# Hybrid diffusion step on one core: the first norm's product taken before the modulations, scale, shift and split after them

## Chip, cores and metric

The kernel runs on one core of one Trainium2 chip. The metric is device microseconds (us) of one execution. A kernel's time is the median of several runs. Before the change it is 1882.99 us, the median of three runs from 1879.08 to 1884.51.

## What is computed

One inference step of a two-layer backbone, for 512 latent tokens and 128 context tokens of width 1024. Each sub-layer takes an RMS norm of the residual stream, then a scale and a shift that come from a conditioning vector through a linear map (the modulations), then a mixer, an output projection and a convolutional gated MLP. The change lies in the first of these norms:

```
def modulation(cvec, w_mod, b_mod):
    m = jax.nn.silu(cvec) @ w_mod + b_mod
    return jnp.split(m[:, None, :], 6, axis=-1)

sh1, sc1, g1, sh2, sc2, g2 = modulation(cvec, p['w_mod'][i], p['b_mod'][i])
h = rmsnorm(x, p['norm_mix'][i]) * (1.0 + sc1) + sh1
# even layer: DeltaNet heads and a Hyena long convolution
proj = h @ p['ev_w_in'][j]
filt = hyena_filters(L, p, j)
```

`rmsnorm` is x times the reciprocal root of the mean square over the 1024 channels, times a gain. The Hyena filters don't depend on the tokens. They come from a small network on positions and are then taken to the frequency domain.

## The kernel before

**Layout.** Channels lie on the 128 partitions and tokens along the free dimension: 642 columns, of which 0 to 511 are latent tokens, 512 and 513 a gap, and 514 to 641 context tokens. The 1024 channels are 8 blocks of 128 (index d), two to a tile, so the input is four tiles `x0`. Work on all tokens is done in two halves, columns 0 to 383 and 384 to 641 (`HALVES`); the second half has two parts with a scale and shift each (`HPARTS`). The large products go three times through TensorE (`mm3`, L310 to L312): the activation and the weight are each split into a rounded high part and the rest, the low part. So each activation needs a high tile (a ScalarE cast, L429) and a low tile (a subtraction, L430).

**The prologue.** L888 makes the generator `filt` of the Hyena filters, and L889 to L912 are the code around the change. A loop of 16 steps takes the shift and scale maps of layer 0 (`mod_chunk`, L212): each step loads 512 KB of `w_mod` and multiplies it by the conditioning columns. In the same loop the four `x0` tiles are loaded, the squares of x are summed over the blocks into `acc` (`sq_acc`, L437 and L440), and `filt` is advanced 12 times. After the loop, `settle` ends the last `mod_finish`: a ScalarE copy (L223), a transpose on TensorE (L227) and the addition of the bias on VectorE (L230). `mod_scale` (L276) makes the scale `scl`. Then for each half:

- `norm_stats`: column sums of `acc` on TensorE (L379), mean and epsilon on VectorE (L392), the power -0.5 on GpSimd (L395), the broadcast over partitions on TensorE (L403), and a ScalarE copy into `rb` (L410, or L414 in the second half);
- `norm_mod` for each of the 8 blocks: x times `rb` on VectorE into a scratch tile `nt` (L421), scale and shift on ScalarE (L427; one instruction in the first half, two in the second), the high cast on ScalarE (L429), and the low subtraction (L430) on VectorE for even blocks and GpSimd for odd ones;
- after every odd block one more step of `filt`, 8 steps in all.

**The filters.** `filt` has 4 steps for the small network and then four blocks of 11 steps. A block has five steps `f3` (two matmuls each, L842 and L843; the decay's products on VectorE, L850, or on ScalarE and GpSimd, L847 and L848; corrections of one row, L853 and L855), one step of butterflies (L769 to L776, `ye` and `yd`), and five steps of the transform `hsp` (L867, L869; L871 and L872 in the last; a small one, `hs`, L878). Each transform step copies its result to `hst` (L873, L881, L882, and a memset, L883) and stores it from ScalarE's queue (L884). `hst` has two buffers.

**What follows.** The coefficients `ab` come from h through a weight of 32 columns (L958). Then the first head pair's six projections (`heads_in(0)`) and the rest of `filt` are merged by their costs, 38.4 * 1.2 against `FW` = 60. When both are done the filters' pool is closed and the pool `dn` of the DeltaNet opens in its place: L1107, L1111 and on write its tiles. Three PSUM banks serve the projections, `f3` and `hsp` alike. Below the code, the framework's scheduler sets the order on each engine from the order of the code and its own costs. Each engine runs its instructions in that order.

Of the kernel before, what the change touches and what calls it, by code (L numbers as in the profile page):

```python
# [11 lines left out]
F32 = mybir.dt.float32  # L12
F32R = mybir.dt.float32r
BF16 = mybir.dt.bfloat16
AF = mybir.ActivationFunctionType
ALU = mybir.AluOpType
# [4 lines left out]
P = 128  # L21
# [5 lines left out]
NT = 642  # L27
PO = 514
COFF = [0, 128, 256, 384, PO]
HALVES = ((0, 384), (384, 642))  # L30
# [5 lines left out]
HPARTS = (((0, 384, 0),), ((384, 512, 0), (PO, NT, 1)))  # L36
# [52 lines left out]
def hybrid_kernel(ctx: ExitStack, tc: tile.TileContext, A, O):  # L89
    nc = tc.nc  # L90
# [17 lines left out]
    def nm(s):  # L108
        uid[0] += 1
        return f"{s}_{uid[0]}"  # L110

    def slot(s, shape=(P, 2, NT), dt=F32, pool=None):
        return (pool or slots).tile(list(shape), dt, tag="slot", name=nm(s))
# [5 lines left out]
    def s_ps(s="sp"):  # L119
        return bank("s", s)  # L120
# [23 lines left out]
    def step():  # L144
        for g in list(pending):
            if next(g, g) is g:
                pending.remove(g)
# [31 lines left out]
    def pc(name, i=0, n=1):  # L179
        a, b = PCOL[name]  # L180
        assert a + i + n <= b
        return par[:, a + i : a + i + n]
# [21 lines left out]
    scl = perm.tile([P, 2, 2, KD, 2], F32, tag="scl", name="scl")  # L204
# [68 lines left out]
    def mod_scale(layer, w):  # L273
        ch = 1 + 3 * w
        gain = pc("norm_mix" if w == 0 else "norm_ffn", 8 * layer, 8)
        nc.vector.scalar_tensor_tensor(  # L276
            out=scl[:, layer, w], in0=mod[:, layer, 8 * ch : 8 * ch + 8, :], scalar=1.0,
            in1=gain[:, :, None].broadcast_to([P, KD, 2]), op0=ALU.add, op1=ALU.mult,
        )

    def mcol(layer, ch, d, m):
        return mod[:, layer, 8 * ch + d, m : m + 1]
# [82 lines left out]
    def new_acc():  # L365
        return tmp.tile([P, NT], F32, tag="acc", name=nm("acc"), bufs=1)


    def norm_stats(acc, rb, hf, last=None, cut=CUT):

        cs = cut[2][hf]
        c0 = cut[0][hf][0]
        n = len(cs)
        ps = s_ps("ss")
        for i, (a, b) in enumerate(cs):
            nc.tensor.matmul(ps[: b - a, i : i + 1], acc[:, a:b], ones, start=True, stop=last is None)  # L379
            if last is not None:  # L380
                nc.tensor.matmul(ps[: b - a, i : i + 1], last[:, a:b], ones, start=False, stop=True)
        v = tmp.tile([P, 3], F32, tag="nv", name=nm("nv"))[:, :n]
        rs = tmp.tile([P, 3], F32, tag="nr", name=nm("nr"))[:, :n]

        runs = []
        for i, (a, b) in enumerate(cs):
            if runs and runs[-1][2] == b - a:
                runs[-1][1] = i + 1
            else:
                runs.append([i, i + 1, b - a])  # L390
        for i, j, h_ in runs:
            nc.vector.tensor_scalar(  # L392
                out=v[:h_, i:j], in0=ps[:h_, i:j], scalar1=1.0 / D, scalar2=EPS, op0=ALU.mult, op1=ALU.add
            )
            nc.gpsimd.tensor_tensor(  # L395
                out=rs[:h_, i:j], in0=v[:h_, i:j], in1=mhalf[:h_].broadcast_to([h_, j - i]), op=ALU.pow
            )
        ps = s_ps("rb")
        if last is not None and cut is SCUT:
            nc.vector.memset(ps[:, 512 - c0 : 514 - c0], 0.0)  # L400
        for i, (a, b) in enumerate(cs):
            h_ = b - a
            nc.tensor.matmul(  # L403
                ps[:, a - c0 : b - c0], rs[:h_, i : i + 1].broadcast_to([h_, P]), ident[:h_, :h_], start=True, stop=True
            )
        if last is not None:
            return ps
        if hf == 0:
            c1 = cut[0][0][1]
            nc.scalar.copy(rb[:, :c1], ps[:, :c1])  # L410
        else:
            nc.gpsimd.memset(rb[:, 512:514], 0.0)
            for a, b, _ in cut[1][1]:
                nc.scalar.copy(rb[:, a:b], ps[:, a - c0 : b - c0])  # L414

    def norm_mod(x, rb, layer, w, act, hf, ds=range(KD)):

        c0, c1 = HALVES[hf]
        for d in ds:
            t = tmp.tile([P, NT], F32, tag="ft" if d % 2 else "fs", name=nm("nt"))  # L420
            nc.vector.tensor_tensor(out=t[:, c0:c1], in0=x[d // 2][:, d % 2, c0:c1], in1=rb[:, c0:c1], op=ALU.mult)  # L421
            for a, b, m in HPARTS[hf]:
                s_, b_ = scl[:, layer, w, d, m : m + 1], mcol(layer, 0 if w == 0 else 3, d, m)
                if layer and not w:
                    nc.vector.tensor_scalar(out=t[:, a:b], in0=t[:, a:b], scalar1=s_, scalar2=b_, op0=ALU.mult, op1=ALU.add)
                else:
                    nc.scalar.activation(t[:, a:b], t[:, a:b], AF.Identity, scale=s_, bias=b_)  # L427
            hi, lo = act.h(d, c0, c1), act.l(d, c0, c1)
            nc.scalar.copy(hi, t[:, c0:c1])  # L429
            (nc.vector if d % 2 == 0 else nc.gpsimd).tensor_tensor(out=lo, in0=t[:, c0:c1], in1=hi.bitcast(F32), op=ALU.subtract)  # L430

    def sq_acc(acc, xt, first, c0=0, c1=NT, last=False):
        if first:
            nc.scalar.activation(acc[:, c0:c1], xt[:, c0:c1], AF.Square)
        else:
            q = tmp.tile([P, NT], F32, tag="fs", name=nm("sq"))
            nc.scalar.activation(q[:, c0:c1], xt[:, c0:c1], AF.Square)  # L437
            if last:
                return q
            nc.vector.tensor_tensor(out=acc[:, c0:c1], in0=acc[:, c0:c1], in1=q[:, c0:c1], op=ALU.add)  # L440
# [293 lines left out]
    x0 = []  # L734
# [53 lines left out]
    fp = filt_stack.enter_context(tc.tile_pool(name="filt", bufs=1))  # L788
# [99 lines left out]
    filt = filters()  # L888
    acc = new_acc()  # L889
    first = mods(((0, 0), (0, 1)), d_ps)  # L890
    for n in range(2 * KD):
        next(first)
        if n % 2 == 0 and n < 8:
            x0.append(slot("x0"))
            nc.sync.dma_start(x0[-1], A["xT"][:, n : n + 2, :])
        if n >= 5 and n < 13:
            d = n - 5
            sq_acc(acc, x0[d // 2][:, d % 2, :], d == 0)
        if n % 2:
            step()  # L900
        if n < 4 or n >= 8:
            next(filt)
    settle()
    mod_scale(0, 0)
    rb = fp.tile([P, NT], F32, tag="z1", name="rb0")
    h = Act("h0", gap=False)
    for hf in range(2):
        norm_stats(acc, rb, hf)
        for d in range(KD):
            norm_mod(x0, rb, 0, 0, h, hf, (d,))  # L910
            if d%2:
                next(filt)  # L912

    def unit_T(idx, j, conv=True):

# [51 lines left out]
    for r in range(2):  # L967
        for j in range(5):
# [3 lines left out]
                out=sp1[:, :, j, r, :], in0=hp2(ps[:, o + 8 : o + 12]), in1=hp2(pc("dn_dt_bias", 4 * r, 4)), op=ALU.add  # L972
# [9 lines left out]
    for hp in range(2):  # L982
        nc.vector.scalar_tensor_tensor(
            out=gg[:, hp].rearrange("p j r h -> p j (r h)"), in0=sp2[:, hp].rearrange("p j r h -> p j (r h)"), scalar=-1.0,
            in1=f4(ea[:, hp])[:, None, :].broadcast_to([P, 5, 4]), op0=ALU.mult, op1=ALU.mult,
# [655 lines left out]
    h = h2  # L1641
# [346 lines left out]
    for i, s_ in enumerate((1, -1)):  # L1988
        nc.gpsimd.affine_select(
            out=band[:, i, :], in_=band[:, i, :], compare_op=ALU.is_ge, fill=fill_neg, base=0,  # L1990
# [192 lines left out]
def build(arrays):  # L2183
    import concourse.bacc as bacc

    nc = bacc.Bacc("TRN2", target_bir_lowering=False, num_devices=1, dynamic_dma_scratch_size=2048)
    A = {
        k: nc.dram_tensor(f"in_{k}", v.shape, mybir.dt.from_np(v.dtype), kind="ExternalInput").ap()
        for k, v in arrays.items()
    }  # L2190
    O = {k: nc.dram_tensor(f"out_{k}", s, F32, kind="ExternalOutput").ap() for k, s in OUTS.items()}
    with tile.TileContext(nc) as tc:
        hybrid_kernel(tc, A, O)
    return nc
# [9 lines left out]
```

## Time and profile before

| | |
|---|---|
| median of three runs | 1882.99 us |
| profiled execution, its own time | 1880.43 us |
| its span | 1878.7 us |
| TensorE busy (PE) | 1788.3 us, 95% |
| VectorE (DVE), ScalarE (ACT), GpSimd (POOL) busy | 1374.1, 848.1, 311.4 us |
| mean granted TensorE clock | 0.98 |
| time from the span's start to `scl` ready | 55.9 us |
| to the first half's first product with `rb` | 59.3 us |
| to the last low tile of h | 90.0 us |

The lines of the profile give start, duration, engine, source line, operation, and output and inputs by the program's names. "x4" after the shapes is the count that a line merges. In square brackets stands how long the engine had been idle and what ended that. In a table by stretches, each row gives the length of the stretch, the busy time of each engine with its count of instructions, the granted TensorE clock (PEclk, 1.00 is full), and the DMA engines' share and rate. PEld is the loading of weights. A matmul of plain 32-bit data leaves two records, one of the rounded kind leaves one.

### The profile page before, as it was taken

Reading aid. Unit: us, or ns where it says so; the run is one execution under the profiler, and the core shown is the slowest. Engines: PE = TensorE matmul, PEld = TensorE weight load, DVE = VectorE, ACT = ScalarE, POOL = GpSimd, SP = SyncE. Lnnn points to the kernel's source line nnn. Section 1 sums busy time; section 2 is a strip of 40 time slices with the busy share of each in tenths; the row PEclk is TensorE's granted clock in tenths of the full one; section 3 lists DMA queues with packets and bytes.
Section 4 is the critical chain, followed back from the end, with each engine's and each line's share of the span. In section 5 each row is a group of like instructions: output and inputs, shape, how many; then the busy total and the mean of one; then the engine's idle time right before and its main releaser. Section 6 shows DMA issues by size and latency. Waiting matters only on the chain.

```text
span 1878.7 us, 31471 instructions
## 1 busy us (share of the span) xinstructions
PE 1788.3 (95%) x12052; PEld 1665.0 (89%) x12052; DVE 1374.1 (73%) x2896; ACT 848.1 (45%) x1678; POOL 311.4 (17%) x349
## 2 busy tenths in 40 slices
PE   5899999999888899999999999999999999999997
PEld 1578999998667899999999998977799999999997
DVE  5755666667887989886887888976778874774874
ACT  3555443433232436633634635445526651552653
POOL 2323442324544210000000003200000000000001
PEclk9899999999989999999999999999999999999999
DMA  8332112224544641555556563411242552552631
GB/s 292 128 104 77 36 57 74 67 72 138 176 168 139 234 141 53 143 186 141 138 183 168 130 217 138 140 53 40 91 180 62 146 152 57 146 139 74 160 90 57
DMA packets 86066, 234.20 MB, mean 125 GB/s; under 512 B 9080, under 2 KB 20728, under 8 KB 85786
## 3 DMA queue, kind: packets, MB, share of 16 engines
q1 hardware_dynamic: 66112, 192.45, 30.9%
q0 software_dynamic: 5760, 20.97, 6.7%
q10 hardware_dynamic: 14042, 18.76, 2.9%
q8 instruction: 95, 1.56, 0.3%
q14 instruction: 57, 0.47, 0.1%
HBM read 215.61 MB, written 16.54 MB: 124 GB/s over the span
## 4 chain that ended last, share of the span: by engine, by line
PE 72%; DVE 13%; ACT 3%; POOL 3%; issue 2%; DMA 2%; POOLq 0%; DVEq 0%; ACTq 0%
PE mm L310 10%; PE mm L312 10%; PE mm L311 10%; PE bx L310 4%; PE bx L311 4%; PE bx L312 4%; PE bv L312 2%; PE bv L310 2%; PE bv L311 2%; PE tr L1009 2%; PE fx L1395 1%; PE YT L1176 1%; PE Y L1174 1%; PE Q L1168 1%; PE o L1872 1%
## 5 line engine op out<-in xcount | busy, mean ns | idle before, releaser
L579 ACT CAST cwh<-wr 128x512 fp32r<-128x512 f32 x200 | 119.6, 621 | 144.8 <-PE bx L311 45.9
L304 ACT CAST wwh<-wr 128x1024 fp32r<-128x1024 f32 (+1 forms) x100 | 101.3, 1013 | 175.8 <-PE mm L311 133.9
L580 DVE TENSOR_TENSOR cwl<-wr,cwh 128x512 fp32r<-128x512 f32 x200 | 133.8, 686 | 36.2 <-ACT cwh L579 36.0
L305 DVE TENSOR_TENSOR wwl<-wr,wwh 128x1024 fp32r<-128x1024 f32 (+1 forms) x100 | 122.2, 1223 | 39.4 <-ACT wwh L304 38.6
L310 PE MATMUL mm<-h0h,wwh 128*128 128x384 f32 (+2 forms) x448 | 148.5, 331 | 0.5 <-DVE d L850 0.2
L446 DVE SCALAR_TENSOR_TENSOR x<-mm,mod,x 128x128 f32<-128x128 f32 (+3 forms) x192 | 77.5, 436 | 95.0 <-PE mm L312 94.8
L311 PE MATMUL mm<-h0l,wwh 128*128 128x384 f32 (+2 forms) x448 | 140.1, 313 | 0.0
L591 POOL DMA_DIRECT2D t<-in_w_up x40 | 34.5, 864 | 633.4 <-DMA t<-in_w_up 150.0
L312 PE MATMUL mm<-h0h,wwl 128*128 128x384 f32 (+2 forms) x448 | 139.3, 311 | 0.0
L257 DVE SCALAR_TENSOR_TENSOR mjunk<-mraw,crow 128x512 f32<-128x512 f32 x192 | 125.3, 685 | 1.9 <-DMA mraw<-in_w_modT 1.4
L310 PE MATMUL od<-owh,h2h 128*128 128x256 f32 x320 | 97.0, 305 | 0.1
L679 DVE SCALAR_TENSOR_TENSOR cv<-ab,par,cv 128x641 f32<-128x641 f32 x88 | 77.7, 883 | 25.2 <-ACT cv L677 24.4
L312 PE MATMUL od<-owh,h2l 128*128 128x256 f32 x320 | 91.5, 289 | 2.1 <-DVE h2l L430 1.3
L311 PE MATMUL od<-owl,h2h 128*128 128x256 f32 x320 | 90.5, 284 | 0.0
L310 PEld LDWEIGHTS mm<-h0h,wwh 128*128 128x128 f32 x448 | 85.3, 190 | 3.7 <-issue 1.8
L1139 POOL TENSOR_TENSOR am<-a,msk 128x512 fp32r<-128x512 f32 x60 | 73.0, 1225 | 92.4 <-PE Q L1168 81.2
L311 PEld LDWEIGHTS mm<-h0l,wwh 128*128 128x128 f32 x448 | 84.8, 189 | 0.5 <-issue 0.2
L312 PEld LDWEIGHTS mm<-h0h,wwl 128*128 128x128 f32 x448 | 84.5, 189 | 0.1
L726 DVE SCALAR_TENSOR_TENSOR cv<-mm,par,cv 128x382 f32<-128x382 f32 (+2 forms) x96 | 52.1, 544 | 32.5 <-ACT cv L720 31.7
L579 ACT CAST cwh<-t 128x512 fp32r<-128x512 f32 x80 | 48.0, 622 | 47.5 <-PE bx L311 17.3
L437 ACT ACTIVATE sq<-x 128x320 f32<-128x320 f32 (+4 forms) x63 | 31.5, 501 | 78.7 <-DVE x L446 64.8
L310 PEld LDWEIGHTS od<-owh,h2h 128*128 128x128 f32 x320 | 60.4, 189 | 4.5 <-issue 4.2
(555 smaller groups left out, 6170.7 us busy)
## 6 DMA issues: line engine op xcount, KB each, us to landing
wr<-in_w_mod SPq DMA_DIRECT2D x48, 512.0 KB, 4.6
wr<-in_w_up SPq DMA_DIRECT2D x48, 512.0 KB, 4.2
mraw<-in_w_modT SPq DMA_DIRECT2D x40, 512.0 KB, 5.5
t<-in_w_up SPq DMA_DIRECT2D x80, 256.0 KB, 3.1
t<-in_w_up POOLq DMA_DIRECT2D x40, 512.0 KB, 5.5
wr<-in_w_in SPq DMA_DIRECT2D x28, 512.0 KB, 3.3
wr<-in_w_dn SPq DMA_DIRECT2D x32, 448.0 KB, 3.5
wr<-in_w_up SPq DMA_DIRECT2D x40, 256.0 KB, 3.7
```

Source lines behind the costliest of these rows:

```text
L257: nc.vector.scalar_tensor_tensor(out=junk, in0=w[:, c : c + 512], scalar=1.0, in1=rows[m][:, c0 + c : c0 + c + 512], op0=ALU.mult, op1=ALU ...
L304: nc.scalar.copy(hi[:, :K], src)
L305: nc.vector.tensor_tensor(out=lo[:, :K], in0=src, in1=hi[:, :K].bitcast(F32), op=ALU.subtract)
L310: nc.tensor.matmul(ps, l[0](k), r[0](k), start=start, stop=False, skip_group_check=more)
L311: nc.tensor.matmul(ps, l[0](k), r[1](k), start=False, stop=False, skip_group_check=more)
L312: nc.tensor.matmul(ps, l[1](k), r[0](k), start=False, stop=stop, skip_group_check=more)
L446: nc.vector.scalar_tensor_tensor(out=xt[:, a:b], in0=ps[:, a - c0 : b - c0], scalar=mcol(layer, ch, d, m), in1=xt[:, a:b], op0=ALU.mult, o ...
L579: nc.scalar.copy(hi, src)
L580: nc.vector.tensor_tensor(out=lo, in0=src, in1=hi.bitcast(F32), op=ALU.subtract)
L679: nc.vector.scalar_tensor_tensor(out=t[:, c0:c1], in0=ar[:, c0 + s_ : c1 + s_], scalar=w[i], in1=t[:, c0:c1], op0=ALU.mult, op1=ALU.add)
L726: nc.vector.scalar_tensor_tensor(out=t[:, c0:c1], in0=p[:, c0 + s_ - a : c1 + s_ - a], scalar=w[i], in1=t[:, c0:c1], op0=ALU.mult, op1=ALU ...
L1139: eng.tensor_tensor(out=v(out), in0=v(a32), in1=msk[:, lv, :, None, :].broadcast_to([P, 2, 2, P]), op=ALU.mult)
```

## The change

In step 13 of the loop, when `acc` is complete, `norm_stats` is now taken for both halves, and each `x0` tile is multiplied by `rb` in place, two blocks to an instruction (L906). `rb` has a tile of its own in the filters' pool (tag `rb0`; before, it used that of `z1`). After `settle` and `mod_scale`, each block is scaled and shifted in place, on VectorE for odd blocks (L923) and on ScalarE for even ones (L925), cast to the high tile on ScalarE (L927), and subtracted for the low tile on VectorE for all blocks (L928). GpSimd has no subtraction left there. The 8 steps of `filt` in this part are gone from it: they follow in the merge with the first head pair's projections.

```diff
+        if n == 13:
+
+            rb = fp.tile([P, NT], F32, tag="rb0", name="rb0")
+            for hf in range(2):
+                norm_stats(acc, rb, hf)
+                c0, c1 = HALVES[hf]
+                for x_ in x0:
+                    nc.vector.tensor_tensor(
+                        out=x_[:, :, c0:c1], in0=x_[:, :, c0:c1], in1=rb[:, None, c0:c1].broadcast_to([P, 2, c1 - c0]), op=ALU.mult
+                    )
         if n % 2:
             step()
         if n < 4 or n >= 8:
             next(filt)
     settle()
     mod_scale(0, 0)
-    rb = fp.tile([P, NT], F32, tag="z1", name="rb0")
     h = Act("h0", gap=False)
     for hf in range(2):
-        norm_stats(acc, rb, hf)
+        c0, c1 = HALVES[hf]
         for d in range(KD):
-            norm_mod(x0, rb, 0, 0, h, hf, (d,))
-            if d%2:
-                next(filt)
+            xd = x0[d // 2][:, d % 2, :]
+            for a, b, m in HPARTS[hf]:
+                s_, b_ = scl[:, 0, 0, d, m : m + 1], mcol(0, 0, d, m)
+                if d % 2:
+                    nc.vector.tensor_scalar(out=xd[:, a:b], in0=xd[:, a:b], scalar1=s_, scalar2=b_, op0=ALU.mult, op1=ALU.add)
+                else:
+                    nc.scalar.activation(xd[:, a:b], xd[:, a:b], AF.Identity, scale=s_, bias=b_)
+            hi, lo = h.h(d, c0, c1), h.l(d, c0, c1)
+            nc.scalar.copy(hi, xd[:, c0:c1])
+            nc.vector.tensor_tensor(out=lo, in0=xd[:, c0:c1], in1=hi.bitcast(F32), op=ALU.subtract)
```

Lines after L912 are 16 higher in the changed kernel (the coefficients' L958 is L974 there).

VectorE's queue around the scale, before (`nv` is the mean, `nt` the scratch tile, `wwl` the low part of a projection's weight):

```order
L776 SCALAR_TENSOR_TENSOR yd_352<-yd_351,d_263 128x256
L883 MEMSET hst_367 1x256
L230 TENSOR_TENSOR mod<-modt_388,par 128x2x4x2
L276 SCALAR_TENSOR_TENSOR scl<-mod,par 128x16
L392 TENSOR_SCALAR nv_414<-ss_410 128x3
L421 TENSOR_TENSOR nt_423<-x_4_113,rb_401 128x384
L421 TENSOR_TENSOR nt_428<-x_4_113,rb_401 128x384
```

VectorE's queue up to the scale, now, from the first half's last product with `rb`:

```order
L906 TENSOR_TENSOR x_25_226<-x_25_226,rb_341 128x2x384
L392 TENSOR_SCALAR nv_362<-ss_359 128x2
L769 TENSOR_TENSOR yd_386<-d_263 128x512
L775 SCALAR_TENSOR_TENSOR yd_387<-yd_386,d_263 128x256
L771 TENSOR_TENSOR yd_386<-yd_386 128x256
L906 TENSOR_TENSOR x_4_113<-x_4_113,rb_341 128x2x258
...
L776 SCALAR_TENSOR_TENSOR yd_387<-yd_386,d_263 128x256
L305 TENSOR_TENSOR wwl_616<-wr_613,wwh_615 128x1024
L883 MEMSET hst_402 1x256
L305 TENSOR_TENSOR wwl_729<-wr_726,wwh_728 128x1024
L230 TENSOR_TENSOR mod<-modt_423,par 128x2x4x2
L276 SCALAR_TENSOR_TENSOR scl<-mod,par 128x16
```

The eight products with `rb`, the seven instructions of `yd` and two splits of weights (L305) now stand ahead of `mod` and `scl`; before, the products and the splits stood behind them, and `yd` ahead.

TensorE's queue before the coefficients, before:

```order
L842 MATMUL f_105_544<-wsh,zs 128x512
L843 MATMUL f_105_544<-wsl,zs 128x512
L379 MATMUL ss_500<-ones,acc_105 128x1 x2
L403 MATMUL rb_507<-ident,nr_504 128x128 x2
L842 MATMUL f_108_561<-wsh,zs 128x512
L843 MATMUL f_108_561<-wsl,zs 128x512
L842 MATMUL f_111_580<-wsh,zs 128x512
L843 MATMUL f_111_580<-wsl,zs 128x512
L958 MATMUL ab_113_610<-h0h_402,wr_592 32x384 x2
```

And now:

```order
L403 MATMUL rb_366<-ident,nr_363 128x128 x2
L869 MATMUL hsp_428<-yd_387,dft_f_256 128x256
L869 MATMUL hsp_403<-yd_386,dft_f_256 128x256
L878 MATMUL hs_68_409<-ye_376,dft_f_256 128x256
L869 MATMUL hsp_403<-yd_387,dft_f_256 128x256
L869 MATMUL hsp_428<-yd_387,dft_f_256 128x256
L227 MATMUL modt_423<-ident,mev_421 128x128 x2
L974 MATMUL ab_83_522<-h0h_436,wr_504 32x384 x2
L310 MATMUL mm_619<-h0h_436,wwh_615 128x384
```

The second filter block's five `f3` steps, which stood ahead of the coefficients, now stand behind them and behind the first projection. The transpose of the scale map (L227) stands behind the four `yd` matmuls of the first block's first two transform steps.

## Prediction

> **What bounds the kernel now.** I read the page first. It gives TensorE, the engine of the matmuls, 95% of the span. So a change gains only where TensorE stands still or runs on a reduced clock. Next I read the table by stretches over the first 200 us, to find where it does either:
>
> ```profile
> PE 1788.3 (95%) x12052; PEld 1665.0 (89%) x12052; DVE 1374.1 (73%) x2896; ACT 848.1 (45%) x1678; POOL 311.4 (17%) x349
> ```
>
> ```profile
> 55.70:70.00 14.30, 9.19 (x40) 6.26 (x38) 8.38 (x16) 11.22 (x22) 3.50 (x4) 0.91 0.41 142
> 70.00:81.00 11.00, 9.72 (x45) 3.99 (x44) 9.12 (x19) 7.08 (x21) 7.91 (x7) 0.50 0.09 33
> 81.00:91.00 10.00, 9.19 (x70) 7.22 (x67) 9.23 (x19) 5.67 (x14) 7.12 (x6) 0.99 0.19 65
> 100.00:105.00 5.00, 2.87 (x17) 2.07 (x16) 2.46 (x12) 4.59 (x7) 0.00 (x0) 1.00 0.12 45
> 110.00:120.00 10.00, 9.50 (x51) 7.06 (x50) 4.65 (x7) 3.30 (x7) 5.80 (x6) 1.00 0.10 39
> 120.00:130.00 10.00, 8.09 (x42) 6.82 (x43) 9.38 (x24) 3.71 (x7) 0.02 (x1) 1.00 0.05 8
> 150.00:160.00 10.00, 8.80 (x45) 7.31 (x44) 9.77 (x22) 1.49 (x3) 4.92 (x4) 1.00 0.15 53
> 160.00:172.00 12.00, 11.76 (x73) 10.74 (x72) 3.48 (x7) 7.10 (x13) 0.00 (x0) 1.00 0.30 97
> 180.00:196.00 16.00, 13.41 (x98) 12.90 (x96) 10.56 (x22) 9.65 (x15) 7.05 (x10) 1.00 0.10 34
> ```
>
> The first number is the stretch's length, the second TensorE's busy time, and the value behind POOL's is the clock. From 55.7 to 91 us TensorE stands still for 5.11 + 1.28 + 0.81 = 7.2 us, and two thirds of its work there run at a mean clock of 0.91 or 0.50. From 100 on the rows leave it idle for 2.13 + 0.50 + 1.91 + 1.20 + 0.24 + 2.59 = 8.6 us. The timeline says what it waits for in the first part:
>
> ```profile
> 46.00 0.81 DVE L440 TENSOR_TENSOR acc<-acc,sq 128x642 f32<-128x642 f32 x1
> 55.74 0.17 DVE L276 SCALAR_TENSOR_TENSOR scl<-mod,par 128x16 f32<-128x16 f32 x1
> 55.76 0.83 PE L379 MATMUL ss<-ones,acc 128*128 128x1 f32 x6
> 59.26 0.56 DVE L421 TENSOR_TENSOR nt<-x,rb 128x384 f32<-128x384 f32 x1 [2.48 <-ACT rb L410]
> 60.61 1.31 ACT L427 ACTIVATE nt<-nt,mod,scl 128x384 f32<-128x384 f32 x2
> 89.14 0.83 POOL L430 TENSOR_TENSOR h0l<-nt,h0h 128x258 fp32r<-128x258 f32 x1
> ```
>
> The sum of squares is complete at 46.8 us, yet the norm starts at 55.8, behind the modulations. The last low tile of h is ready at 89.97, and the first projection's second half and the coefficients need it.
>
> **The norm moved forward.** From the column sums to the first product with `rb` it takes 59.26 - 55.76 = 3.5 us. Started at 46.8, the first product can run at 50.3. VectorE fills that wait with the `ye` butterflies, so nothing is lost there.
>
> **The products.** Sixteen products become eight of double width. No row has 768 or 516 elements; these stand around them:
>
> ```profile
> L305 DVE TENSOR_TENSOR wwl<-wr,wwh 128x1024 fp32r<-128x1024 f32 x1 | 1.2, 1220 | 0.0
> L769 DVE TENSOR_TENSOR ye<-e 128x512 f32<-128x512 f32 x1 | 0.7, 673 | 0.0
> L774 DVE SCALAR_TENSOR_TENSOR ye<-ye,e 128x256 f32<-128x256 f32 x1 | 0.4, 407 | 0.0
> ```
>
> On the line between the first two a product takes 0.95 us for 768 elements and 0.68 for 516 (bounds 0.67 and 1.22, 0.41 and 0.67). Four of each make 6.5 us.
>
> **What they delay.** VectorE runs in order, and ahead of `mod` and `scl` now stand the eight products (6.5), the seven instructions of `yd` (0.67 + 6 x 0.41 = 3.1, less overlaps with the next of some 0.06: 2.7), two weight splits (2.4), a memset and small steps (0.9), and about 1.0 of waiting for the second half's `rb`, whose mean stands behind the first four products. 50.3 + 13.5 = 63.8: `scl` comes at 63.8 instead of 55.9. The modulations are no longer late by their transfers; they are late because their last addition queues behind the products. The transpose that feeds it (L227) also waits on TensorE for `yd`.
>
> **Scale, shift, split.** ScalarE loses half of L427 to VectorE:
>
> ```profile
> L427 ACT ACTIVATE nt<-nt,mod,scl 128x128 f32<-128x128 f32 x16 | 7.2, 488 | 1.9 <-DVE nt L421 1.9
> L427 ACT ACTIVATE nt<-nt,mod,scl 128x384 f32<-128x384 f32 x8 | 5.4, 704 | 0.0
> L429 ACT CAST h0h<-nt 128x384 fp32r<-128x384 f32 x8 | 3.9, 507 | 0.0
> L429 ACT CAST h0h<-nt 128x258 fp32r<-128x258 f32 x8 | 3.2, 396 | 0.0
> ```
>
> ```profile
> L425 DVE TENSOR_SCALAR nt<-nt,scl,mod 128x384 f32<-128x384 f32 x8 | 4.1, 538 | 0.0
> L425 DVE TENSOR_SCALAR nt<-nt,scl,mod 128x128 f32<-128x128 f32 x16 | 5.2, 380 | 0.0
> L430 DVE TENSOR_TENSOR h0l<-nt,h0h 128x384 fp32r<-128x384 f32 x4 | 2.2, 548 | 0.0
> ```
>
> Now ScalarE does 4 x 0.70 + 8 x 0.51 + 8 x 0.49 + 8 x 0.40 = 14.0 us. In a row they overlap (two of 0.70 took 1.31 together above); at 0.06 for each of 28 it is 12.4, with nothing in between. VectorE does 4 x 0.54 + 8 x 0.38 + 8 x 0.55 + 8 x 0.41 = 12.9 (the last 0.41 is the 256-wide row's), less its overlaps, so ScalarE sets the pace. h is complete at 63.8 + 12.4 + 0.5 = 76.7, 13.3 us earlier than 89.97.
>
> **TensorE behind it.** What it can do from 65.3 on, priced from these rows:
>
> ```profile
> 65.29 0.50 PE L842 MATMUL f<-wsh,zs 128*128 128x512 f32 x1 [2.46 <-ACT hst L873]
> 65.72 0.50 PE L843 MATMUL f<-wsl,zs 64*128 64x512 f32 x1
> 75.70 1.51 PE L958 MATMUL ab<-h0h,wr 128*32 128x384 f32 x8
> 81.48 0.34 PE L312 MATMUL mm<-h0h,wwl 128*128 128x384 f32 x1
> 81.65 0.34 PE L310 MATMUL mm<-h0h,wwh 128*128 128x384 f32 x1
> 88.50 0.62 PE L958 MATMUL ab<-h0l,wr 128*32 128x258 f32 x8
> 88.94 0.62 PE L958 MATMUL ab<-h0h,wr 128*32 128x258 f32 x8
> ```
>
> ```profile
> 163.27 0.86 PE hsp L867 x4
> ```
>
> Starts tell the price: 0.43 per `f3` matmul, 0.17 per projection matmul of 384 columns, 0.44 per eight coefficient matmuls of 258 columns (1.28 per eight of 384 at half clock, so 0.64 at full), 0.43 per transform instruction (two records). The coefficients make 2.6 + 1.8, the first projection's first half 24 x 0.175 = 4.2, two transform steps 8 x 0.43 = 3.4: 12.0 us. TensorE is sparse before 65, so it starts on half clock. I allow 5 us of that, which cost 2.5: 65.3 + 12.0 + 2.5 = 79.8. Before, the same work ended at about 91 (the last low tile at 89.97, then the last coefficients), so 11.2 us are won.
>
> These rows speak for that much half clock, with TensorE busy all the time:
>
> ```profile
> 74.00:76.00 2.00, 2.00 (x7) 0.77 (x10) 1.92 (x3) 1.73 (x6) 2.00 (x3) 0.50 0.00 0
> 80.00:82.00 2.00, 2.00 (x13) 1.03 (x6) 1.46 (x3) 0.76 (x3) 1.71 (x3) 0.72 0.00 0
> ```
>
> The Trainium skill, "TensorE: Matmul & The Clock Gate", Part 1, says that about 3.4 us of sustained activity restore the full clock. The trace disagrees where the 32-column coefficients run: the row from 70 to 81 has TensorE busy for 9.72 of 11 us at a clock of 0.50. By the rule the half clock would cost an estimated 1.7 instead of 2.5, and the gain below would be 0.8 larger.
>
> **What is owed.** Before, by 91 us TensorE had also done the second filter block's five `f3` steps (10 x 0.43 = 4.3), three instructions of the first block's last transform step (1.3) and five of the second block's (2.1). That is 7.7 us, now done later. The lead is 11.2 - 7.7 = 3.5 us.
>
> **Afterwards** the 8.6 us of idle time may shrink or grow. VectorE gets back about 8 us of decay products and butterflies: where it was nearly full (9.38 and 9.77 of 10 us) TensorE lost 1.91 and 1.20, about 0.16 per us of VectorE's work, so 8 us would cost 1.3. On the other side the owed 7.7 us of matmuls can fill idle time. I take the two as cancelling; ends: -1.3 and +7.7. GpSimd only loses work, so nothing waits for it longer. SP's queue keeps its order; its load of the next projection's weight waits for the buffer that the coefficients hold, and comes earlier with them. After the first DeltaNet round both orders are the same, so the lead is carried to the end.
>
> Sum: 1880.43 - 3.5 = 1876.9 us against the profiled execution. The median lies 1882.99 - 1880.43 = 2.56 above it: 1879.5.
>
> **Rivals.** *A, larger gain.* The owed matmuls go into the idle time that is there anyway, as whole projections now stand ready beside them. For it: 8.6 us idle. Against: much of that waits for VectorE chains of the same filters. With half of it filled the gain is 3.5 + 4.3 = 7.8: 1875.2 on the median. With all of the 7.7 it is 11.2: 1871.8.
>
> *B, slower.* The last filter block ends too late. The DeltaNet's tiles wait for the last store of `hst`:
>
> ```profile
> 173.32 0.33 ACTq L884 DMA_DIRECT2D hs<-hst  x1
> 176.10 1.19 POOL L1205 TENSOR_TENSOR dt<-vtok,beta 128x256 f32<-128x256 f32 x2 [21.18 <-DVE cv L726]
> 195.73 1.09 PE L1168 MATMUL Q<-dz,am 128*128 128x128 f32 x8
> ```
>
> From that store's issue to the first `Q` it takes 22.4 us. TensorE bridges them with the 103 projection matmuls that stand in its queue after the block (at 0.15 some 15.5 us) and smaller work, and is idle for 2.6. In the new order 90 stand there, and the last ten transform instructions come in one run instead of spaced by projections, through two store buffers (two stores take about as long as two steps). If the chain keeps its 22.4, 13 x 0.15 = 2 us of cover are gone; if the bunched stores push it back by two more of 2.8 us (173.32 to 176.10), 5.6 more; with three such waits of 1.3 at the other blocks the loss is 11.5. It is a loss once these waits exceed the 3.5 of lead. Price: +8.0, 1891.0 on the median; with the first two alone +4.1, 1887.1. Against it: the first matmuls of that round, `F` and `G`, now stand ahead of the last block's transforms, so a part of the chain is done early.
>
> *C, nothing moves.* The products on VectorE take longer than I priced (1.22 each, +3.9), `scl` comes at 67.7 and h at 80.6; TensorE follows at 82 to 83.7: gain 0, 1883.0.
>
> **Chances.** 0.3%, about what a measurement of this kernel can tell from no change, is 5.6 us. My forecast and C lie within it: 0.36 and 0.12. A, with gains over 5.6, gets 0.40, because 8.6 us of idle time is much and 7.7 us of ready work fits it. B gets 0.12. So 0.40 faster, 0.48 the same, 0.12 slower. The forecast has the most single weight in its band, so the time is 1879.5. The range reaches into A up to 11.2 us of gain and into B up to 4.1 of loss: 1871.8 to 1887.1. The likeliest case's own range, gains of 2.2 to 4.3, is 1878.7 to 1880.8.
>
> **What would show it.** Right: the first double-width product at about 50, 0.95 us long; `scl` at 63 to 64 behind two L305; last L928 before 78; coefficients done near 80; TensorE's idle time from there to the first `Q` near 8.6; that `Q` at about 192. Wrong: `scl` before 60 (the queue doesn't hold it), an idle time far from 8.6, or a store of `hst` more than 2 us later against the projections.

## The result

The changed kernel is slower: 1891.01 us, median of 5 runs (1888.67 to 1892.28), against 1880.07 us of the kernel before in 5 runs beside it (1879.07 to 1884.51). The ratio is 1.0052, with a 95% interval of 1.0036 to 1.0068, so about 9.8 us are lost. The profiled execution took 1892.27 us with a span of 1890.5, 11.8 more than the 1878.7 of before.

### The profile after

The page's head and its first row:

```profile
span 1890.5 us, 31467 instructions
...
PE 1798.0 (95%) x12052; PEld 1674.0 (89%) x12052; DVE 1373.3 (73%) x2908; ACT 844.6 (45%) x1666; POOL 306.4 (16%) x341
```

TensorE runs the same 12052 matmuls as before, and is busy with them for 9.7 us longer (1798.0 against 1788.3). So the same matmuls took longer. That is the first hint.

The timeline after (start, duration, engine, line, operation):

```profile
52.64 0.96 DVE L906 TENSOR_TENSOR x<-x,rb 128x768 f32<-128x768 f32 x1 [0.22 <-ACT rb L410]
...
65.15 0.18 DVE L276 SCALAR_TENSOR_TENSOR scl<-mod,par 128x16 f32<-128x16 f32 x1
...
76.44 0.77 DVE L928 TENSOR_TENSOR h0l<-x,h0h 128x258 fp32r<-128x258 f32 x2 [0.62 <-ACT h0h L927]
...
84.79 0.93 PE L981 MATMUL ab<-sel,ab 128*128 128x16 f32 x7
85.57 0.48 PE L842 MATMUL f<-wsh,zs 128*128 128x512 f32 x1
...
207.66 0.53 PE L1184 MATMUL Q<-dz,am 128*128 128x128 f32 x3
```

and the row of before that closes the coefficients there:

```profile
93.31 0.48 PE L965 MATMUL ab<-sel,ab 128*128 128x16 f32 x3
```

The prologue did what it was meant to do: h is complete at 77.2 (before 89.97), the coefficients at 85.7 (before 93.8). But the first `f3` of the second filter block follows only then, and the first `Q` comes at 207.66 instead of 195.73. The lead is gone, and 12 us with it, inside some 120 us.

To measure it I take the first `R`, the first matmul behind which both programs have issued the same work (528 projection matmuls among it). These are its rows in the views of one line, before and after; the first start is 242.33 and 254.25:

```profile
L1185 PE MATMUL R<-dz,a x80: 270/275/377, 242.3 to 588.7; 128*128 128x128 f32 x80
```

```profile
L1201 PE MATMUL R<-dz,a x80: 271/275/377, 254.2 to 601.0; 128*128 128x128 f32 x80
```

So `R` is 11.9 us late, the whole difference of the spans. TensorE in two windows, before and then after (length, busy time with the count of matmuls, granted clock, DMA share, GB/s):

```profile
46.00:84.00 38.00, 30.63 (x145) 0.82 0.40 135
84.00:242.33 158.33, 148.18 (x965) 1.00 0.22 75
```

```profile
46.00:84.00 38.00, 30.41 (x178) 0.91 0.44 151
84.00:254.25 170.25, 159.03 (x941) 0.94 0.20 69
```

Idle time is length less busy time: 10.2 before, 11.2 after. The clock's loss is busy time times what the clock lacks: 0 before, 159.03 x 0.06 = 9.5 after (9.8 when summed over windows of 2 us, which I use from here on). What remains is work at full clock: 148.2 and 149.2. So of the 11.9 us, some 9.8 are half clock, 1.0 is idle time, and 1.0 is work, by which the kernel after lies *behind* at 84 us. The 9.8 is an upper estimate: it takes every matmul as twice as long at half clock, while projection matmuls of 384 columns start every 0.32 us there (from 194.1 on) and every 0.18 at full clock. By that ratio it is 8.9, and the work 1.9.

Where the half clock comes from shows in windows of 1 us of the kernel after:

```profile
132.00:133.00 1.00, 0.37 (x1) 1.00 0.39 82
133.00:134.00 1.00, 0.00 (x0) 1.00 0.92 369
134.00:135.00 1.00, 0.35 (x3) 1.00 0.19 74
135.00:136.00 1.00, 1.00 (x8) 1.00 0.00 0
136.00:137.00 1.00, 1.00 (x7) 0.53 0.00 0
137.00:138.00 1.00, 1.00 (x6) 0.50 0.00 0
138.00:139.00 1.00, 1.00 (x5) 0.50 0.00 0
139.00:140.00 1.00, 1.00 (x5) 0.76 0.00 0
140.00:141.00 1.00, 1.00 (x6) 1.00 0.00 0
```

TensorE is idle for 2.28 us, works at full clock for a while, and then runs at half clock for 3.5 us, though it is busy all the time. Between 84 us and `R` the kernel after has five such stretches (read in windows of 0.25 us): 105.25 to 112.25, 136.0 to 139.5, 180.25 to 184.0, 194.0 to 197.5 and 214.5 to 218.0. The profile of before has none there, with an idle time that is hardly smaller. Its longest gaps:

```profile
100.00:102.00 2.00, 0.69 (x5) 1.00 0.24 91
...
192.00:194.00 2.00, 0.54 (x4) 1.00 0.00 0
194.00:196.00 2.00, 1.57 (x15) 1.00 0.00 0
```

What TensorE waits for, from 84 us to the first `R` (total, times, longest), after and then before (`khtok`, `rk`, `rq`, `F`, `Q` and `R` belong to the first round of the DeltaNet):

```profile
PE tr L1025 <- POOL khtok L1065: 2.3, 1, 2.3
PE hsp L867 <- DVE ye L771: 2.0, 2, 1.8
PE hsp L869 <- DVE yd L771: 1.8, 1, 1.8
...
PE hsp L867 <- ACT hst L881: 0.9, 1, 0.9
```

```profile
PE tr L1009 <- DVE dx L1147: 2.6, 2, 1.9
PE gc L991 <- ACT spfs L979: 2.1, 1, 2.1
PE hsp L867 <- DVE d L850: 1.7, 1, 1.7
```

The wait for `ye` ends at 102.7 and that for `yd` at 178.4; the stretches of 7.0 and 3.75 us follow 2.5 and 1.9 us later. Those two waits are for butterflies, the steps between a block's `f3` and its transforms. The third, for `khtok`, is the gap at 132. GpSimd stands in two of the three chains, in the timeline of the kernel after:

```profile
130.61 2.86 POOL L194 TENSOR_TENSOR rk<-ss,mhalf 128x10 f32<-128x10 f32 x1
...
172.82 4.73 POOL L770 TENSOR_TENSOR yd<-d 128x512 f32<-128x512 f32 x1
...
177.59 0.43 DVE L775 SCALAR_TENSOR_TENSOR yd<-yd,d 128x256 f32<-128x256 f32 x1 [1.16 <-POOL yd L770]
...
178.40 0.92 PE L869 MATMUL hsp<-yd,dft_f 128*128 128x256 f32 x3 [1.84 <-DVE yd L771]
```

and the same subtraction of the last block before:

```profile
153.45 1.47 POOL L770 TENSOR_TENSOR yd<-d 128x512 f32<-128x512 f32 x1
```

From 173.07 to 176.42 VectorE runs nine instructions of 256 to 512 columns back to back, and beside them GpSimd's subtraction takes 4.73 us instead of 1.47. VectorE then waits 1.16 us for it, and TensorE 1.84 for VectorE. The Trainium skill, "GPSIMD Engine Reference", section 8 (Key points), says that GpSimd shares its SBUF interfaces with VectorE and contends with VectorE's instructions that have two inputs in SBUF; these nine are such instructions, and the trace agrees. It is no single case: in seven of the twelve profiles that have this subtraction on GpSimd, one of the four for `yd` takes 4.5 to 4.8 us, and in the other five the longest takes 1.8.

### The profile page after: what moved, and what is told of

It is laid out like the page before. It is cut to its first block, busy times and chain, and to the rows that moved or that the text cites. A ratio compares the mean times of both kernels' runs of the same rounds, so it can differ in the third digit from the quotient of the medians.

```text
span 1890.5 us, 31467 instructions
## 1 busy us (share of the span) xinstructions
PE 1798.0 (95%) x12052; PEld 1674.0 (89%) x12052; DVE 1373.3 (73%) x2908; ACT 844.6 (45%) x1666; POOL 306.4 (16%) x341
## 4 chain that ended last, share of the span: by engine, by line
PE 69%; DVE 15%; DMA 4%; issue 4%; POOL 4%; ACT 3%; SPq 0%; POOLq 0%; DVEq 0%; ACTq 0%
PE mm L310 9%; PE mm L312 9%; PE mm L311 9%; PE bx L310 4%; PE bx L312 4%; PE bx L311 4%; PE bv L312 2%; PE bv L310 2%; PE bv L311 2%; PE tr L1025 2%; DVE mjunk L257 2%; DMA wr<-in_w_up 1%; PE fx L1411 1%; PE YT L1192 1%; PE Y L1190 1%
## 5 line engine op out<-in xcount | busy, mean ns | idle before, releaser
L305 DVE TENSOR_TENSOR wwl<-wr,wwh 128x1024 fp32r<-128x1024 f32 (+1 forms) x100 | 121.3, 1214 | 27.9 <-ACT wwh L304 27.1
L726 DVE SCALAR_TENSOR_TENSOR cv<-mm,par,cv 128x382 f32<-128x382 f32 (+3 forms) x96 | 51.4, 542 | 46.0 <-ACT cv L720 45.4
```

What stands on the lines that cost most here:

```text
L305: nc.vector.tensor_tensor(out=lo[:, :K], in0=src, in1=hi[:, :K].bitcast(F32), op=ALU.subtract)
L726: nc.vector.scalar_tensor_tensor(out=t[:, c0:c1], in0=p[:, c0 + s_ - a : c1 + s_ - a], scalar=w[i], in1=t[:, c0:c1], op0=ALU.mult, op1=ALU ...
```

## The experiments

Two halves of the change can be told apart: the new norm, and the eight filter steps that its loop no longer takes. "Filter theory" is the second, "norm theory" the first. Ratios are to the kernel before in the same session. The mean clock is the granted clock over the whole execution, averaged over all the runs of a row (for before, 99 runs of four sessions); 0.001 of it is up to 1.9 us. The last three columns are of the profiled execution, up to the first `R`.

| run | ratio, 95% interval | mean clock | first `R` | idle from 84 | lost to half clock |
|---|---|---|---|---|---|
| before | 1 | 0.983 | 242.33 | 10.2 | 0.0 |
| after | 1.0052 (1.0036 to 1.0068) | 0.979 | 254.25 | 11.2 | 9.8 |
| e1 steps back | 0.9981 (0.9972 to 0.9990) | 0.985 | 243.67 | 10.6 | 0.0 |
| e2 before without steps | 1.0058 (1.0042 to 1.0074) | 0.977 | 254.48 | 13.5 | 10.2 |
| e3 filters' share up | 1.0043 (1.0024 to 1.0062) | 0.980 | 252.78 | 11.4 | 7.3 |
| e4 half of the steps | 1.0065 (1.0042 to 1.0089) | 0.978 | 255.67 | 12.1 | 7.9 |
| e5 keep busy | 1.0038 (1.0023 to 1.0052) | 0.982 | 249.66 | 7.7 | 3.4 |
| e6 wider gap | 1.0013 (1.0000 to 1.0025) | 0.982 | 251.08 | 10.5 | 7.8 |
| e7 steps back, wider gap | 0.9984 (0.9971 to 0.9998) | 0.984 | 240.31 | 9.9 | 0.0 |
| e8 twelve steps | 1.0037 (1.0022 to 1.0051) | 0.979 | 251.00 | 9.9 | 4.5 |
| e9 before, keep busy | 1.0015 (1.0001 to 1.0030) | 0.982 | 245.81 | 7.7 | 0.0 |
| e10 VectorE butterflies | 1.0004 (0.9990 to 1.0018) | 0.982 | 243.67 | 7.6 | 3.2 |
| e11 busy elsewhere | 1.0085 (1.0065 to 1.0105) | 0.979 | 259.67 | 10.0 | 10.5 |
| e12 steps back, VectorE | 0.9961 (0.9947 to 0.9975) | 0.985 | 237.58 | 4.9 | 0.0 |
| e13 before, VectorE | 0.9984 (0.9967 to 1.0001) | 0.982 | 239.46 | 6.5 | 0.0 |

The first `R` tells most of the time: 0.001 of the ratio is 1.9 us, and by that the two columns mostly agree within 4 us. The largest difference is e6's: 8.8 us late at `R`, 2.4 by the ratio. A single profile places a kernel no better, since the part behind `R` differs too (1636.4 us in the profile of before, 1629.7 in that of e6), and 35 runs of the kernel before reached from 1873.4 to 1885.1. Most of that difference is half clock as well: without it the part behind `R` takes 1610 to 1615 us in all fifteen profiles. The column of the mean clock doesn't hang on one profile, and it orders the kernels much as the last column does.

### e1 and e2: the two halves apart

```diff
+            if d % 2:
+                next(filt)
```

at the end of the new loop of the kernel after, and for e2 the same two lines taken out of the kernel before.

> The kernel after, with the eight filter steps put back into the new loop (one after each odd block, as the kernel before had them). If the loss is owed to the eight steps that were taken out of the prologue (filter theory), the second filter block's f3 matmuls run again before 84 us, the last hs of the last filter block moves from 188.3 back to 171 to 176, the first Q from 207.7 to 190 to 197, and the median from 1891.0 to 1874 to 1882. If the loss is owed to the norm part itself (products ahead of scl on VectorE, scl at 65.2 instead of 55.7, lows all on VectorE), putting the steps back changes little: the median stays at 1888 to 1893, or goes above it because VectorE has more to do in the same stretch.

> The kernel before, with nothing changed but that its norm loop takes no filter steps; the eight then follow in the merge with the first head's inputs. It is the one half of the change alone. Filter theory: the last filter block's last hs comes at 186 to 192 instead of 171.8, the first Q at 205 to 212 instead of 195.7, and the median at 1888 to 1896, though the norm is the old one. Norm theory: 1878 to 1884, as the kernel before; a little better if anything, since VectorE is freed of the filters' work in the norm loop.

TensorE from 84 us to the first `R`, e1 and then e2:

```profile
84.00:243.67 159.67, 149.11 (x975) 1.00 0.21 71
```

```profile
84.00:254.48 170.48, 156.99 (x945) 0.93 0.21 73
```

The steps alone make the whole loss: e2 is 1.0058 with the old norm, and half clock costs it 10.2 us. With them back, e1 is even 0.9981. The product of the two, 1.0039, lies within the interval of the change as a whole. The filter theory holds and the norm theory falls. The last `hs` of the last block came at 174.1 in e1 and at 192.7 in e2, the latter just past its range, as was e1's first `Q` (197.1). What the norm does in e1 is worth a look:

```profile
88.35 0.75 DVE L928 TENSOR_TENSOR h0l<-x,h0h 128x258 fp32r<-128x258 f32 x2
...
92.15 1.04 PE L983 MATMUL ab<-sel,ab 128*128 128x16 f32 x8
```

With the steps in the loop, h is complete at 89.1 and the coefficients at 93.2, as before (89.97, 93.8). The time that the earlier norm seemed to free was the time of the steps.

### e3 and e4: the share, and half of the steps

```diff
-FW = 60
+FW = 77
```

for e3, and for e4 the two lines of e1 with `if d % 2 and hf == 1:`.

> The kernel after, with the merge's weight of the filters FW raised from 60 to 77: the eight more steps that are left then take the same part of the first head's projections as before, so that the filters end at the same projection unit. If it is the late end of the filters against the projections that costs (share theory), the first Q goes from 207.7 to 198 to 202 and the median to 1881 to 1886. If it is the amount of filter work that must be done after 84 us, whose VectorE chains TensorE waits for, a greater share packs the chains closer and lengthens the waits: 1889 to 1894. Norm theory: no change, 1889 to 1892.

> The kernel after, with four of the eight filter steps put back, those of the second half of the columns alone. Filter theory, with the loss in proportion to the steps that are missing: half of what putting back all eight gives, 1882 to 1887. If instead there is a threshold (the first f3 steps of the second block, which open the chain of its butterflies), four steps give nearly all of it: within 2 us of the run with all eight. Norm theory: 1888 to 1892.

A line of e4's waits of TensorE from 46 to 92 us:

```profile
PE f L842 <- ACT hst L873: 7.5, 1, 7.5
```

e3 came to 1.0043 (1885.27 us). Its time lies in the range of the share theory, but its first `Q`, 206.1, lies far outside, and its interval overlaps with that of the kernel after. So the filters' late end against the projections is not shown to be a cause; it can be a part. In e4 neither expectation of the filter theory came true: four steps give back nothing (1.0065). The norm theory's 1888 to 1892 took in its 1889.76, but e1 and e2 speak against that theory. In the second half of the loop the first `f3` waits 7.5 us for the copy of a transform that stands on ScalarE behind the whole first half of the norm, and everything behind it on TensorE waits along. By this one run, the number of steps alone does not count; where they stand against the norm in each queue does.

### e5, e9 and e11: is it the clock?

```diff
+                    if g == 0 and hf + o:
+                        for _ in range(10):
+                            nc.tensor.matmul(ps, zs[:, 0:128], wsh[:, 0, 0, :], start=True, stop=True)
```

ahead of the transforms, in the kernel after (e5) and in the kernel before (e9); with `g == 4` in the kernel after (e11). The real transform overwrites what these matmuls leave.

> The kernel after, with ten extra matmuls of 512 columns (about 0.21 us each at full clock) ahead of the first transform of each of the last three filter blocks; their result is overwritten, nothing else changes. They take 6.5 us of TensorE in all and run where TensorE waits for the butterflies (2.0 and 1.8 us in the kernel after). Clock theory (9.8 of the 11.8 us by which the kernel after falls behind between 84 us and the first R are matmuls at half clock, which follow upon these waits): the half clock after 84 us falls from 9.8 to below 4, the first R comes at 247 to 252 instead of 254.25 in spite of the added work, and the ratio to the kernel before falls to 1.000 to 1.003. If the loss is the waiting and the order alone and the clock only goes along with it: the half clock stays above 7, and the time goes up by the 2 to 4 us of added work that no wait covers, ratio 1.006 to 1.008.

> A control for the run that keeps TensorE busy: the kernel before with the same ten extra matmuls ahead of the first transform of each of the last three filter blocks. Clock theory: the kernel before has no half clock between 84 us and the first R, so the extra 6.5 us only cost, less the 1 to 2 us of waits for ye that they cover: half clock there stays below 2, the first R comes at 245 to 248 instead of 242.33, ratio to before 1.0015 to 1.0035. If extra matmuls help in general (a filled wait, a clock held up somewhere later): ratio 1.000 or below.

> A second control: the kernel after with the same number of extra matmuls in the same three blocks, but ahead of each block's last transform instead of its first, where TensorE does not wait. Clock theory, with the covered waits as the reason: the half clock after 84 us stays at 7 to 12 and the extra matmuls are paid for at their full price, first R at 259 to 262, ratio to before 1.007 to 1.010. If extra matmuls hold the clock up wherever they stand: half clock below 5, first R at 250 to 256, ratio below 1.006.

TensorE from 84 us on in e5, e9 and e11:

```profile
84.00:249.66 165.66, 158.02 (x967) 0.98 0.20 70
```

```profile
84.00:245.81 161.81, 154.13 (x998) 1.00 0.22 73
```

```profile
84.00:259.67 175.67, 165.65 (x964) 0.93 0.19 66
```

More work at the right place brings `R` earlier. In e5 TensorE does some 5.4 us more work (154.6 against 149.2 at full clock) and reaches `R` 4.6 us earlier: idle time falls by 3.5 and half clock by 6.4. The same matmuls where nothing waits (e11) cost 5.4 us at `R`, and the half clock stays at 10.5. In the kernel before, which has no half clock to lose, they cost 3.5. Against the kernel after the gain of e5 is not clear of the noise (1.0038 and 1.0052, intervals that overlap). What is clear is e5 against e11, the same work in two places: 1.0038 and 1.0085, at a mean clock of 0.982 and 0.979. All three came as the clock theory had them, but for e5's ratio: 1.0038, above the expected 1.0030, with 1.0030 within its interval. So most of the half clock is a consequence of the waits ahead of it, and it, not the idle time as such, is the larger part of the loss.

### e6 and e7: a wider gap in the merge

```diff
-FW = 60
+FW = 70
...
-                yield 1.6
+                yield 4.8
```

The second edit is behind the butterflies; e7 is e1 with the same, and FW 73.

> The kernel after, with the weight of the butterfly step raised from 1.6 to 4.8 in the merge, so that about 2.5 us more of projections stand between a block's last f3 step and its first transform; FW is raised from 60 to 70 so that the filters end at the same part of the first head's inputs. Clock theory with the waits for the butterflies as its cause: TensorE's waits for ye and yd (4 us between 84 and 208) go to below 1.5, the half clock after 84 us from 9.8 to below 5, first R at 245 to 250, ratio to before 1.000 to 1.003. If the loss comes from the total of filter work that is left for the merge, wherever it stands: waits appear elsewhere (f for hst, transforms for d) and the ratio stays at 1.004 to 1.006.

> The kernel after with the eight filter steps back in the loop (0.9981 of the kernel before when measured alone), and with the same wider gap after the butterflies (4.8 for 1.6, FW 73 for 60 to keep the filters' end). If the remaining waits of 1.6 to 1.7 us for ye and d are on the path: ratio to before 0.995 to 0.998. If there TensorE's idle time before the first R is only moved: 0.998 to 1.000. If the later end of a block's transforms delays the stores that the first DeltaNet round needs: above 1.000.

e6 is faster, 1.0013, but not for the reason expected: TensorE's waits for `yd` grew from 1.8 to 4.6 us, the half clock stays at 7.8, and `R` is only 3.2 us earlier. Most of the gain lies behind `R`: 6.5 us against the kernel after, of which 4.4 are half clock (16.9 against 21.3, summed as above). No run shows whether the edit did that or chance. It tells little on the cause. e7 (0.9984) equals e1: where no half clock follows, moving the waits gains nothing.

### e8: more steps ahead of the merge

```diff
-        if n < 4 or n >= 8:
-            next(filt)
+        next(filt)
```

in e1.

> The kernel after with the eight filter steps back in the loop, and four more taken in the fifth to eighth step of the modulation loop, where the kernel before takes none, so that 24 instead of 20 steps run ahead of the merge. Filter theory carried on (steps ahead of the merge fill TensorE's dead time, steps in the merge are paid for): the last hs of the last block comes 5 to 8 us earlier than the 174.1 of the run with eight, and the ratio to before falls to 0.994 to 0.998. If the dead time of the prologue is used up, or VectorE's queue there is full: 0.998 to 1.001. If the steps push the squares and the norm back: above 1.001.

A line of TensorE's waits from 46 to 92 us:

```profile
PE hsp L867 <- DVE ye L771: 15.2, 2, 12.6
```

1.0037: this rival of the expectation is right, the steps push the norm back. `scl` comes at 74.4, the coefficients end at 102.6, and one transform waits 12.6 us for butterflies that stand in VectorE's queue among the norm. The last `hs` is no earlier either, 174.6.

### e10, e12 and e13: butterflies on VectorE

```diff
-                ye = butterflies("ye", e_, nc.gpsimd)
-                yd = butterflies("yd", d_, nc.gpsimd)
+                ye = butterflies("ye", e_, nc.vector)
+                yd = butterflies("yd", d_, nc.vector)
```

in the kernel after (e10), in e1 (e12) and in the kernel before (e13).

> The kernel after with the subtraction of each butterfly step on VectorE instead of GpSimd (eight instructions, 4.73 us for one of them on GpSimd at 172.82 against 1.4 for others); nothing else is changed. If GpSimd's part in the chain is what TensorE waits for: the waits for yd (1.8 us at 178, 2.1 at 71) go to below 0.5, the half clock after 84 us falls from 9.8 by about 2.5 for each wait of over 1.5 us that goes, to 4 to 7, first R at 247 to 251, ratio to before 1.000 to 1.003. If it is VectorE's queue (the decay products and butterflies stand behind the heads' work there), the waits stay or move to ye: ratio 1.004 to 1.006.

> The kernel after with the eight filter steps back in the loop (0.9981 of before when measured) and the butterflies' subtraction on VectorE. A try to beat both kernels. If the waits of 1.6 us for ye and 1.7 for d there are GpSimd's: first R 1 to 3 us earlier than 243.67, ratio to before 0.9965 to 0.9980. If VectorE, with the added 8 times 0.6 us in and after the norm loop, delays the norm's lows instead: 0.998 to 1.001.

> The kernel before, with its old norm, and the butterflies' subtraction on VectorE instead of GpSimd. If the norm part of the change is worth nothing by itself and the gain of the run with the steps back and VectorE's butterflies (0.9961) is owed to the butterflies alone: ratio 0.995 to 0.997. If the norm part is worth the 3.5 us that the run with the steps back showed (0.9981): this kernel gains only the other half, 0.9975 to 0.999. If the old norm's loop, which has GpSimd take part of the lows, suffers from more work on VectorE: 1.000 or above.

e10 in its timeline (the subtraction that took GpSimd 4.73 us), then e10, e12 and e13 from 84 us on:

```profile
170.27 0.67 DVE L770 TENSOR_TENSOR yd<-d 128x512 f32<-128x512 f32 x1
```

```profile
84.00:243.67 159.67, 152.01 (x938) 0.98 0.20 71
```

```profile
84.00:237.58 153.58, 148.64 (x975) 1.00 0.22 74
```

```profile
84.00:239.46 155.46, 148.98 (x978) 1.00 0.23 76
```

e10 gives nearly all of the loss back, more than expected: `R` at 243.67, half clock 3.2, ratio 1.0004. Two waits remain, 2.4 us for `khtok` and 1.5 for `yd`, which was expected below 0.5. So GpSimd's part of the chain is much of what made the butterflies late. e12 is faster than both kernels: 1871.24 us median, 0.9961, both it and its `R` a little better than expected. e13, the old norm with the same butterflies, is 0.9984 with 1 just within its interval; that is the case in which the norm half is worth something by itself. The norm half is worth 0.0019 by e1 against before and 0.0023 by e12 against e13, some 4 us, though the intervals of the latter two overlap. In e1 it does not show ahead of `R` (1.3 us later than before), in e12 it does (1.9 earlier than e13). The mean clock says what they are: 0.985 in e1 and e12 against 0.982 in the runs of before beside e1 and in e13, some 5 us of the span. Why this norm brings less half clock stays open.

## Why the prediction was wrong

**VectorE's queue: right.** The first wide product came at 52.6 instead of 50.3, since `rb`, for which its row waits, came later; the products took 0.89 and 0.63 us, priced at 0.95 and 0.68 by an estimate; `scl`, held by them, came at 65.15 instead of 63.8; h was complete at 77.2, forecast 76.7. Rival C falls with that; its sum was off besides, as eight products of 1.22 us are 3.3 us more than 6.5, not 3.9.

**TensorE behind it: too much won.** I had the coefficients, the projection's half and the transforms done at 79.8; they were done at 85.6. The work was priced at 12.0. In the window from 65.3 to 85.6 TensorE was busy 18.66 of 20.30 us, of which 4.27, from 66.94 to 71.21, were at half clock. That cost 2.1 (2.5 allowed), so the work was 16.5 at full clock. By the starts of the matmuls, the coefficients took 6.2 where 4.4 stood in the sum, the projection's half 5.0 for 4.2, the transforms 4.3 for 3.4 (three steps stood there, not two), and the `ab<-sel` matmuls, which were left out, 1.0. The gain was 8.1, not 11.2, and with what was owed the lead of 3.5 was not there at all: at 84 us the kernel after lay some 1.0 us of work behind.

**"Afterwards": the step that failed.** The prediction took VectorE's relief and the owed matmuls "as cancelling; ends: -1.3 and +7.7". It counted idle time alone and took the full clock for granted, as the rows that it shows from 100 us on have it, 1.00 in each. Idle time did cancel almost (11.2 against 10.2). What came on top was up to 9.8 us of half clock. The term should have been a price per wait: a gap of about 2 us costs itself and, where a half clock follows, up to 1.75 us (half of 3.5) or 3.5 (half of 7.0) more.

**What was owed was priced as work only.** The eight steps are a chain over four engines. In the norm's loop their waits lay where TensorE waited anyway; before and after, it was idle for 7.4 and 7.6 us from 46 to 84, and in e1 for 6.4. In the merge the same chains stand between projections that are in a fixed proportion to them, and TensorE's queue, which is in order, stops at each late butterfly.

**Rival B** named the right sign and by accident the right time (1891.0), with 0.12. Its mechanism was not the one: the last block did end 16.6 us later, at 188.9, but from there to the first `Q` it took 18.8 us, less than before (22.4 from the store's issue, 23.5 from the last `hs`). "GpSimd only loses work, so nothing waits for it longer" is refuted by the subtraction of 4.73 us and by e10.

The Trainium skill, "TensorE: Matmul & The Clock Gate", section "HAM oscillation — how this bites in real kernels", warns of idle gaps over about 3.4 us. In this kernel gaps of 1.8 to 2.3 us were enough for a half clock, so the measurement decides. The same page's Part 1 says that the activity window is 3413 ns long and runs freely. The stretches here, 3.5, 7.0 and 10.5 us in nearly all the profiles, are multiples of about that, and the trace agrees. How gaps of 2 us can do it is shown under the last heading.

## What to carry to other kernels

Work taken out of another engine's waiting time isn't free where it goes to: price its chain of waits there, not only its matmuls. Where a window shows the full clock, ask how far it is from losing it; a wait of 2 us may cost as much again in the work behind it. To tell waiting from a lowered clock, split the window into idle time, clock loss and work at full clock, and put harmless work into the wait, and as a control where nothing waits: if the first is faster than the second and the clock loss falls, it was the clock.

## What the runs showed of the hardware that was not expected

- Half clock comes in whole stretches and late: 3.5, 7.0 or 10.5 us, mostly beginning within 3 us after a gap's end, while TensorE is busy again. The same gap does not always bring it: 2.28 us at 132 in the kernel after did, 2.09 at 100.5 in the kernel before and 2.25 at 187.5 in e12 did not.
- The clock goes by a grid of steps. In the kernel after the five stretches begin at 105.34, 136.06, 180.43, 194.09 and 214.57 us, which lie 9, 13, 4 and 6 steps of 3.413 us apart, and the starts in every other profile fit such a grid. Cut by it, the gap at 132 leaves 2.00 us of idle time in one step (132.65), while the gap of before is split by the border at 101.58, and the step behind it has 1.24:

```profile
132.65:136.06 3.41, 1.41 (x9) 1.00 0.44 154
136.06:139.47 3.41, 3.41 (x14) 0.50 0.00 0
```

```profile
98.17:101.58 3.41, 2.52 (x17) 1.00 0.20 77
101.58:105.00 3.42, 2.18 (x12) 1.00 0.03 13
```

  From 84 us to the first `R`, in all fifteen profiles, each of the 15 steps at full clock with 1.8 us or more of idle time was followed by half clock; the most idle time in a step that was not is 1.71. The other 13 stretches follow steps with 0 to 1.6 us of idle time. So it is partly luck how a gap falls on the grid. This is read from the traces; no run moved a gap on purpose.
- Stretches also came with no idle time in the 4 us ahead of them (194.0 in the kernel after, 192.0 in e6, 199.75 in e11). There the step ahead holds twenty matmuls of a single column, which the profile counts as busy:

```profile
190.83 2.29 PE L1092 MATMUL rq<-ones,qs 128*128 128x1 f32 x20
```

  Twenty of them in a row stand in six profiles. In four they lie within one step, with half clock behind (e5 is the fourth); in e2 and e10 a border splits them, and in the other nine profiles they come ten and ten, all without it. So a busy TensorE with next to nothing to do counted like an idle one.
- A GpSimd subtraction of 512 columns took 1.47 us, and 4.73 beside a dense run of small VectorE instructions; one of ten columns (`rk`) took 1.95 or 2.86.
